# Moving twenty subtractions from VectorE to GpSimd in the attention of a hybrid decoder

## The chip, the cores and the metric

The kernel runs on one core of one Trainium2 chip. The metric is the device time of one execution in microseconds; lower is better. A core has five engines with queues of their own, each worked through in order: PE (TensorE, matrix products and transposes), DVE (VectorE), ACT (ScalarE), POOL (GpSimd) and SP (here only DMA issues). An instruction that needs another engine's result waits for a semaphore and holds up all that is queued behind it on its own engine.

## The reference

Two layers over 512 tokens of width 1024, all in float32. Layer 0 is a gated short convolution and a squared-ReLU MLP. Its result is normalised and projected once to keys and values. Layer 1 is a sparse attention with 16 heads in 4 groups, each head 64 wide, and another MLP. The attention has three branches that share the queries: compressed blocks, selected blocks and a window. With 512 tokens the selection takes all blocks, so both of the latter are full causal attention. Cut to the attention:

```
logit_c = einsum('bqghd,bngd->bqghn', qt, k_cmp) + bias_c         # 31 compressed keys
p_c = softmax(where(valid_c, logit_c, NEG_INF)) * has_any
o_c = einsum('bqghn,bngd->bqghd', p_c, v_cmp)
...                                                               # the same for selection and window
o = gt[..., 0:1] * o_c + gt[..., 1:2] * o_s + gt[..., 2:3] * o_w
x = x + o.reshape(B, S, N_HEADS * HEAD_DIM) @ w_o
```

v_cmp comes out of a small MLP (phi) over blocks of 32 tokens: `silu(flat @ w1) @ w2`.

## The kernel before

Each float32 operand of a product is split into two float16 pieces, the high one rounded from the value and the low one the remainder. A product is then three matmuls: high by high, high by low, low by high (`mm3`, lines 356 to 359). The splitting costs two elementwise instructions for each operand: ACT writes the high piece, and DVE subtracts it from the value (`split_to`, lines 377 to 382). Weights arrive by DMA in pieces (`wst`), and are split ahead of their use in the same way (lines 203 and 204).

The kernel is written for a tile scheduler: the order within each engine's queue and the semaphores come out of its plan, from the order in which the program states the work, the buffers that a tile name has (`bufs`) and what the planner holds each instruction to cost.

The attention is a list of items. A `Full` item is one group, one block of 128 queries, one branch (selection or window) and one to four heads; a `Cmp` item is two groups and one block of 128 queries in the compressed branch. There are 8 `Cmp` items: four for groups 0 and 1, put into the items of group 2, and four for groups 2 and 3, put into those of group 3. Each item has five stages, which the main loop states some items apart (`lead = {1: 2, 2: 3, 3: 4, 4: 6}`):

- st0: the logits on PE into bank "b"; DVE adds the bias into `at_s` (3 buffers), and ACT takes the exponential into `at_p`. A `Full` item gets sum and minimum in one DVE instruction (line 1021). A `Cmp` item adds (1089), reduces to the maximum (1091), subtracts it (1092), then exponential (1097) and sum (1099).
- st1: PE transposes the probabilities into one of two "c" banks (lines 1029, 1104); ACT copies the high piece out (1032, 1108).
- st2: DVE makes the low piece (1035, 1111), after which the bank is free.
- st3: the product with the values (1048 to 1050, 1120 to 1122), and its scaling by DVE into `o_t` (966), which POOL adds to the output `o` (968, 971).
- st4: where both parts of a group's block are there, `finish` has PE transpose `o` into a "c" bank (982), and `split_to` makes the pieces of the turned output in the tile `big` (378 and 380). `finish` handles one group, 256 columns, or two at once, 512. `finished` counts the blocks done of each group.

Between the items a background generator runs the projections: raw keys and values, `phi`, the queries of groups 1 to 3 (`queries`, where DVE scales them at line 703, ACT makes the high pieces at 800 and POOL the low ones at 801), and the output projection of groups 0 and 1 once all their blocks are finished. The output projection of groups 2 and 3 closes the attention. At the end of `phi(1)` the compressed values are spread over four heads by a mask (892) and split into `VC` by `split_to`.

Of the kernel before, what the change touches and what calls it, by code (L numbers as in the profile page):

```python
# [10 lines left out]
F32 = mybir.dt.float32  # L11
F16 = mybir.dt.float16
AF = mybir.ActivationFunctionType
OP = mybir.AluOpType
# [34 lines left out]
def body(ctx, tc, x, rel_bias, norm_mix, norm_mlp, mlp_w1, mlp_w2, a_w_in, a_conv_w, a_w_out,  # L49
# [3 lines left out]
    PE, ACT, DVE, POOL = nc.tensor, nc.scalar, nc.vector, nc.gpsimd  # L53
# [11 lines left out]
    def bank(tag, shape=(128, 512)):  # L65
        n = {"a": 2, "b": 2, "c": 2, "d": 1, "e": 1}[tag]
        return psum.tile(list(shape), F32, name=tag, bufs=n)
# [159 lines left out]
    def drain(gen):  # L227
        for _ in gen:
            pass
# [144 lines left out]
    def ftile(name, bufs=2, n=S):  # L374
        return wk[0].tile([128, n], F32, name=name, bufs=bufs)

    def split_to(hi, lo, src, scale=1.0):
        ACT.activation(hi, src, AF.Copy, scale=scale)
        if scale == 1.0:
            DVE.tensor_tensor(lo, src, hi, op=OP.subtract)  # L380
        else:
            DVE.scalar_tensor_tensor(lo, src, scale, hi, op0=OP.mult, op1=OP.subtract)
# [24 lines left out]
    for p in range(4):  # L407
# [55 lines left out]
        for dst in (pc, pu, pb):  # L463
# [7 lines left out]
            for m in range(2):  # L471
                ch = 2 * p + m
                if dst is pc:
                    if m == 0:
                        tmps = []
                    t = ftile("cv_t", 2)
# [177 lines left out]
    with pool("attn") as ap:  # L654
# [8 lines left out]
        VC = ap.tile([128, 2, G, 4, 64], F16, name="VC")  # L663
# [169 lines left out]
        def phi(which):  # L833
            kr = KRs[which]
            ph = [bank("a"), bank("a")]
            for quarter in range(4):
                w = next_piece()
                cv = ahead_fine()
                for c in range(4):
                    cc = 4 * quarter + c  # L840
                    at = 64 * (cc % 8) + cc // 8
                    rhs = [kr[:, hl, 0:5, at:at + 31] for hl in range(2)]
                    for m in range(2):
                        o = ph[m][:, 0:155].rearrange("p (g j) -> p g j", g=5)
                        mm3(o, [u[:, c, m * 128:(m + 1) * 128] for u in w], rhs, cc == 0, cc == 15)
                        next(cv, None)
                    yield 0.42
                drain(cv)
            hs = ap.tile([128, 2, 2, G, 32], F16, name="phi_h", bufs=1)
            DVE.memset(hs[:, :, :, :, 31:32], 0.0)  # L850

            for m in range(2):
                bias = ap.tile([128, 2], F32, name="phi_b", bufs=2)
                ACT.activation(bias[:, 0:1], ph[m][:, 124:125], AF.Copy)
                ACT.activation(bias[:, 1:2], ph[m][:, 124:125], AF.Copy, scale=0.5 / (SW * SK))
                t = ap.tile([128, G, 31], F32, name="phi_t", bufs=2)
                v = ph[m][:, 0:124].rearrange("p (g j) -> p g j", g=4)
                ACT.activation(t, v, AF.Tanh, bias=bias[:, 1:2], scale=0.5 / (SW * SK))
                ACT.activation(t, t, AF.Identity, bias=ones)
                DVE.scalar_tensor_tensor(t, v, bias[:, 0:1], t, op0=OP.add, op1=OP.mult)  # L860
                split_to(hs[:, m, 0, :, 0:31], hs[:, m, 1, :, 0:31], t, 0.5 * SR / (SW * SK))
            for _ in range(4):
                yield
            w = next_piece()
            if which == 0:
                pk = bank("e")
                w2 = [ap.tile([128, 2, 2, 64], F16, name=f"phi_w2{i}") for i in range(2)]
                for i in range(2):
                    for d in range(2):
                        DVE.tensor_copy(w2[i][:, :, d], w[i])  # L870
                for m in range(2):
                    mm3(pk[:, 0:128], [u[:, m].rearrange("p a b -> p (a b)") for u in w2],
                        [hs[:, m, i].rearrange("p g j -> p (g j)") for i in range(2)], m == 0, m == 1)
                split_to(KC[:, 0], KC[:, 1], pk[:, 0:128].rearrange("p (g j) -> p g j", g=4), SK / (SR * SW))
                yield
            else:
                pv = bank("e")
                hd = ap.tile([128, 4, S], F16, name="kr_hl", bufs=1).rearrange(
                    "p (m i) (g h n) -> p m i g h n", m=2, g=G, h=4)
                for m in range(2):  # L880
                    for i in range(2):
                        DVE.tensor_copy(hd[:, m, i], hs[:, m, i][:, :, None, :].to_broadcast([128, G, 4, 32]))
                for g in range(4):
                    o = pv[:, g * 64:(g + 1) * 64]
                    for m in range(2):
                        lh = [hd[:, m, i, g].rearrange("p h n -> p (h n)") for i in range(2)]
                        PE.matmul(o, lh[0], w[0][:, m], start=m == 0, stop=False)
                        PE.matmul(o, lh[0], w[1][:, m], start=False, stop=False)
                        PE.matmul(o, lh[1], w[0][:, m], start=False, stop=m == 1)
                for g in range(4):  # L890
                    t = ftile("at_s", 3)[:, 0:256].rearrange("p (h d) -> p h d", h=4)
                    DVE.tensor_tensor(t, pv[:, None, g * 64:(g + 1) * 64].to_broadcast([128, 4, 64]),
                                      hmask[:, :, None].to_broadcast([128, 4, 64]), op=OP.mult)
                    split_to(VC[:, 0, g], VC[:, 1, g], t)
                yield
            drain(ahead())

# [75 lines left out]
        def finish(g, n, qb, tag="c"):  # L973

            nonlocal ot
            if ot is None:
                o16 = ap.tile([128, 2, 8, S], F16, name="big", bufs=1)
                ot = (o16[:, 0], o16[:, 1])
            p = bank(tag)
            for j in range(n):  # L980
                for i in range(2):
                    PE.transpose(p[:, (2 * j + i) * 128:(2 * j + i + 1) * 128],
                                 og[g // 2, qb][:, (g + j) % 2, i * 128:(i + 1) * 128], ident)
            d = [u[:, 2 * g:2 * (g + n), qb * 128:(qb + 1) * 128] for u in ot]
            split_to(d[0], d[1], p[:, 0:n * 256].rearrange("p (i q) -> p i q", i=2 * n))
            for j in range(n):
                finished[g + j] += 1
            if finished[0] == finished[1] == 4:
                done.add("o1")

        finished = [0] * 4
# [74 lines left out]
        class Cmp:  # L1066
# [8 lines left out]
            def st0(self):  # L1075
                gp, qb, n = self.gp, self.qb, self.n
                if (gp, qb) == (0, 3):
                    done.add("cmp0")
                s = bank("b")[:, 0:256].rearrange("p (h n) -> p h n", h=8)
                for j in range(8):  # L1080
                    g, h = 2 * gp + j // 4, j % 4
                    q = Qs[g][:, h, qb * 128:(qb + 1) * 128]
                    PE.matmul(s[:, j, :n], q, KC[:, 0, g, :n], start=True, stop=False)
                    PE.matmul(s[:, j, :n], q, KC[:, 1, g, :n], start=False, stop=True)
                lg = ftile("at_s", 3)[:, 0:256].rearrange("p (h n) -> p h n", h=8)
                i = 8 * qb + 7
                tc_ = TC[gp].rearrange("p g h n -> p (g h) n")
                tv = tc_[:, :, i::-1] if i - n < 0 else tc_[:, :, i:i - n:-1]
                DVE.tensor_tensor(lg[:, :, :n], s[:, :, :n], tv, op=OP.add)
                mx = ap.tile([128, 8], F32, name="c_m", bufs=2)  # L1090
                DVE.tensor_reduce(mx, lg[:, :, :n], axis=mybir.AxisListType.X, op=OP.max)
                DVE.tensor_tensor(lg[:, :, :n], lg[:, :, :n], mx[:, :, None].to_broadcast([128, 8, n]),
                                  op=OP.subtract)
                self.p = ftile("at_p", 3)[:, 0:256].rearrange("p (h n) -> p h n", h=8)
                if n < 32:
                    POOL.memset(self.p[:, :, n:], 0.0)
                ACT.activation(self.p[:, :, :n], lg[:, :, :n], AF.Exp, bias=zero, scale=1.0 / SL)
                self.l = ap.tile([128, 8], F32, name="c_l", bufs=4)
                DVE.tensor_reduce(self.l, self.p[:, :, :n], axis=mybir.AxisListType.X, op=OP.add)
# [109 lines left out]
    with pool("hidden_b") as hp:  # L1209
# [5 lines left out]
        for half in range(2):  # L1215
            nc.gpsimd.dma_start(fng[half], bass.AP(tensor=final_norm.tensor, offset=final_norm.offset + half * S,
                                                   ap=[[0, 128], [1, S]]))
# [159 lines left out]
```

## Time and profile before

| | us |
|---|---|
| runs before, median of 3 (lowest to highest) | 1114.18 (1113.89 to 1116.89) |
| the profiled execution | 1114.68 |
| its span, first to last instruction | 1112.8 |
| PE, DVE, ACT, POOL busy | 1093.5, 869.8, 572.5, 62.4 |

The first half of the span, to about 530 us, is layer 0. The attention lies from about 530 to 790 us, and the second MLP behind it. A row of a wait reads: who waited, for whom, total us, how often, the longest. A group row reads: source line, engine, operation, output and inputs by the program's names, shapes, count; busy time in us and mean ns of one; idle time of the engine just before them and what ended it. A timeline row reads: start, duration, engine, line, operation; in brackets the idle time before it. A stretch row has, for each engine, the busy us and the number of instructions, and then the granted TensorE clock (1.00 is full), the busy share of the DMA engines and GB/s. PE's matmuls overlap and their ends are modelled.

### The profile page before, as it was taken

What the parts mean: (1) busy time and instruction counts of PE and PEld (TensorE: products, weight loads), DVE (VectorE), ACT (ScalarE), POOL (GpSimd) and SP (SyncE); (2) the same over time, 40 slices, a digit from 0 to 9 for tenths busy, and PEclk for the clock granted to TensorE, in tenths of its full rate; (3) what the DMA queues carried; (4) which work ended last, traced back from release to release, by engine and by line L of the source; (5) the groups of instructions that cost most, each with busy time, mean ns of one, the idle gap of its engine ahead of it and who ended that gap; (6) DMA issues with size and microseconds to landing.
All of it is one profiled execution on the core that took longest, in us unless ns stands there. A gap on an engine that the chain in (4) does not pass through costs nothing.

```text
span 1112.8 us, 20136 instructions
## 1 busy us (share of the span) xinstructions
PE 1093.5 (98%) x8004; PEld 696.9 (63%) x8004; DVE 869.8 (78%) x1630; ACT 572.5 (51%) x923; POOL 62.4 (6%) x79
## 2 busy tenths in 40 slices
PE   9999999999999999999998999899999999999997
PEld 4444444446884448875767676676444788444896
DVE  5755457987988677969588889897998698865876
ACT  4522235555343444447578787775755434343353
POOL 1000000000000000000102021212000000000021
PEclk9999999999999999999999999999999999999999
DMA  6433335543334333313334241111653333330221
GB/s 215 133 97 102 107 96 151 155 129 100 110 117 121 102 96 107 103 34 108 117 97 135 69 127 59 39 39 58 189 152 114 96 114 114 114 95 1 86 86 77
DMA packets 149565, 115.75 MB, mean 104 GB/s; under 512 B 8684, under 2 KB 146624, under 8 KB 149472
## 3 DMA queue, kind: packets, MB, share of 16 engines
q1 hardware_dynamic: 146624, 109.14, 32.3%
q10 hardware_dynamic: 2464, 4.70, 1.4%
q8 instruction: 63, 1.03, 0.4%
q0 software_dynamic: 384, 0.63, 0.2%
q14 instruction: 30, 0.25, 0.1%
HBM read 110.22 MB, written 2.14 MB: 101 GB/s over the span
## 4 chain that ended last, share of the span: by engine, by line
PE 86%; DVE 7%; ACT 4%; issue 2%; POOL 1%; DMA 1%; SPq 0%; DVEq 0%; ACTq 0%
PE a L583 8%; PE c L583 7%; PE a L358 6%; PE a L359 6%; PE a L357 6%; PE b L583 6%; PE c L359 6%; PE c L358 6%; PE c L357 6%; PE b L359 6%; PE b L358 5%; PE b L357 5%; PE d L583 4%; PE e L583 2%; PE c L1029 2%
## 5 line engine op out<-in xcount | busy, mean ns | idle before, releaser
L203 ACT ACTIVATE whi<-wst 128x1024 f16<-128x1024 f32 (+3 forms) x172 | 144.3, 854 | 188.0 <-PE b L358 66.8
L204 DVE SCALAR_TENSOR_TENSOR wlo<-wst,whi 128x1024 f16<-128x1024 f32 (+3 forms) x172 | 170.0, 999 | 44.8 <-ACT whi L203 44.3
L583 PEld LDWEIGHTS <-whi 128*128 128x128 f16 x1768 | 173.0, 98 | 20.5
L359 PEld LDWEIGHTS <-wlo 128*128 128x128 f16 x1024 | 100.3, 98 | 111.5 <-issue 0.5
L358 PEld LDWEIGHTS <-whi 128*128 128x128 f16 x1024 | 100.2, 98 | 108.7 <-issue 2.8
L357 PEld LDWEIGHTS <-whi 128*128 128x128 f16 x1024 | 100.3, 98 | 107.7 <-issue 0.9
L190 ACT ACTIVATE whi<-wst 128x1792 f16<-128x1792 f32 x64 | 108.5, 1700 | 109.5 <-DVE wst L188 47.5
L191 DVE SCALAR_TENSOR_TENSOR wlo<-wst,whi 128x1792 f16<-128x1792 f32 x64 | 129.3, 2023 | 14.0 <-ACT whi L190 14.0
L188 DVE TENSOR_TENSOR wst<-wst 128x256 f32<-128x256 f32 x256 | 96.1, 428 | 20.1 <-DMA wst<-mlp_w_dram 18.5
L534 DVE TENSOR_TENSOR rl<-ml_z,rh 128x1792 f16<-128x1792 f32 x32 | 64.8, 2026 | 44.7 <-ACT rh L533 44.7
L583 PEld LDWEIGHTS <-wlo 128*128 128x128 f16 x884 | 86.5, 98 | 10.5 <-issue 0.2
L533 ACT ACTIVATE rh<-ml_z 128x1792 f16<-128x1792 f32 x32 | 54.3, 1696 | 57.3 <-DVE ml_z L532 57.3
L1023 ACT ACTIVATE at_p<-at_s,at_m 128x384 f32<-128x384 f32 (+3 forms) x128 | 70.8, 554 | 22.2 <-DVE at_m L1021 20.7
L359 PE MATMUL b<-xsh,wlo 128*128 128x512 f16 x208 | 78.8, 379 | 0.0
L358 PE MATMUL b<-xsl,whi 128*128 128x512 f16 x208 | 78.8, 379 | 0.0
L357 PE MATMUL b<-xsh,whi 128*128 128x512 f16 x208 | 78.7, 379 | 0.0
L357 PE MATMUL c<-xsh,whi 128*128 128x512 f16 x192 | 72.8, 379 | 0.0
L358 PE MATMUL c<-xsl,whi 128*128 128x512 f16 x192 | 72.8, 379 | 0.0
L359 PE MATMUL c<-xsh,wlo 128*128 128x512 f16 x192 | 72.8, 379 | 0.0
L583 PE MATMUL a<-rh,whi 128*128 128x256 f16 x256 | 69.1, 273 | 0.0
L583 PE MATMUL a<-rh,wlo 128*128 128x256 f16 x256 | 69.1, 273 | 0.0
L583 PE MATMUL c<-rh,wlo 128*128 128x256 f16 x252 | 68.7, 273 | 0.0
(329 smaller groups left out, 2570.7 us busy)
## 6 DMA issues: line engine op xcount, KB each, us to landing
wst<-mlp_w_dram SPq DMA_DIRECT2D x256, 256.0 KB, 3.4
wst<-a_w_in_dram SPq DMA_DIRECT2D x18, 512.0 KB, 3.6
wst<-w_kv_dram SPq DMA_DIRECT2D x12, 512.0 KB, 3.5
T<-ext_d ACTq DMA_DIRECT2D x4, 1056.0 KB, 5.8
wst<-a_w_out_dram SPq DMA_DIRECT2D x8, 512.0 KB, 3.4
wst<-b_w_qg_dram SPq DMA_DIRECT2D x8, 512.0 KB, 3.6
wst<-b_w_o_dram SPq DMA_DIRECT2D x8, 512.0 KB, 3.4
wst<-a_w_in_dram SPq DMA_DIRECT2D x7, 384.0 KB, 4.8
```

Source lines behind the costliest of these rows:

```text
L188: DVE.tensor_tensor(b[:, :, o], b[:, :, x], b[:, :, y], op=e)
L190: ACT.activation(hi, b[:, :, 1:], AF.Copy, scale=sc)
L191: DVE.scalar_tensor_tensor(lo, b[:, :, 1:], sc, hi, op0=OP.mult, op1=OP.subtract)
L203: ACT.activation(hi[:, s:e], w, AF.Copy, scale=sc)
L204: DVE.scalar_tensor_tensor(lo[:, s:e], w, sc, hi[:, s:e], op0=OP.mult, op1=OP.subtract)
L357: PE.matmul(ps, w[0], xs[0], start=start, stop=False)
L358: PE.matmul(ps, w[0], xs[1], start=False, stop=False)
L359: return PE.matmul(ps, w[1], xs[0], start=False, stop=stop)
L533: ACT.activation(rh[0][:, p], z[:, 1:8], AF.Copy)
L534: DVE.tensor_tensor(rh[1][:, p], z[:, 1:8], rh[0][:, p], op=OP.subtract)
L583: mm = PE.matmul(acc7[i], wl if n == 1 else wh, xl if n == 2 else xh, stop=c == closes[i] and n == 2, start=c == 0 and n == 0 and not othe ...
L1023: ACT.activation(self.p[:, w], lg[:, w], AF.Exp, bias=mn[:, j:j + 1], scale=-1.0, accum_out=l[:, br * 4 + h:br * 4 + h + 1])
```

## The change

Three places.

- The low halves of the compressed values: POOL subtracts instead of DVE. ACT's high half stays.
- The low halves of the turned outputs in `finish`: unless the pair of groups (0 and 1, or 2 and 3) has with this call more than 6 of its 8 blocks done, ACT writes the high piece, then a second copy of the values in float32 to a new tile `o_f` with one buffer, and POOL subtracts. The later calls of a pair keep the old way. The count is raised before the test.
- The subtraction of the row maximum in the compressed items: POOL instead of DVE.

```diff
@@ -891,7 +891,8 @@
                     DVE.tensor_tensor(t, pv[:, None, g * 64:(g + 1) * 64].to_broadcast([128, 4, 64]),
                                       hmask[:, :, None].to_broadcast([128, 4, 64]), op=OP.mult)
-                    split_to(VC[:, 0, g], VC[:, 1, g], t)
+                    ACT.activation(VC[:, 0, g], t, AF.Copy)
+                    POOL.tensor_tensor(VC[:, 1, g], t, VC[:, 0, g], op=OP.subtract)
                 yield
@@ -982,9 +983,17 @@
             d = [u[:, 2 * g:2 * (g + n), qb * 128:(qb + 1) * 128] for u in ot]
-            split_to(d[0], d[1], p[:, 0:n * 256].rearrange("p (i q) -> p i q", i=2 * n))
             for j in range(n):
                 finished[g + j] += 1
+            src = p[:, 0:n * 256].rearrange("p (i q) -> p i q", i=2 * n)
+            pair_of = finished[g // 2 * 2:g // 2 * 2 + 2]
+            if sum(pair_of) > 6:
+                split_to(d[0], d[1], src)
+            else:
+                t = ap.tile([128, 512], F32, name="o_f", bufs=1)[:, 0:n * 256].rearrange("p (i q) -> p i q", i=2 * n)
+                ACT.activation(d[0], src, AF.Copy)
+                ACT.activation(t, src, AF.Copy)
+                POOL.tensor_tensor(d[1], t, d[0], op=OP.subtract)
             if finished[0] == finished[1] == 4:
                 done.add("o1")
@@ -1089,8 +1098,8 @@
                 DVE.tensor_reduce(mx, lg[:, :, :n], axis=mybir.AxisListType.X, op=OP.max)
-                DVE.tensor_tensor(lg[:, :, :n], lg[:, :, :n], mx[:, :, None].to_broadcast([128, 8, n]),
-                                  op=OP.subtract)
+                POOL.tensor_tensor(lg[:, :, :n], lg[:, :, :n], mx[:, :, None].to_broadcast([128, 8, n]),
+                                   op=OP.subtract)
                 self.p = ftile("at_p", 3)[:, 0:256].rearrange("p (h n) -> p h n", h=8)
```

In the built program the order of all engines is the same up to the compressed values and again after the attention; in between the scheduler states PE's, DVE's and ACT's instructions in another order.

## The prediction

> **What bounds the kernel now.** First the page: span and busy time by engine.
>
> ```profile
> span 1112.8 us, 20136 instructions
> PE 1093.5 (98%) x8004; PEld 696.9 (63%) x8004; DVE 869.8 (78%) x1630; ACT 572.5 (51%) x923; POOL 62.4 (6%) x79
> ```
>
> TensorE (PE) bounds the whole: 98% busy. The change adds or removes no matmul (the built program only reorders them from the first compressed item on), so it can only move time in which PE waits, or runs at a lower clock. It touches the attention from the compressed values on, whose first low half starts at 674.2 us, to the last moved output, turned at 759.83 (both rows below). The second view is the busy time by stretch, cut there and around the one dip that the page's slices hide.
>
> ```profile
> core 0: us, PE busy (x) PEld busy (x) DVE busy (x) ACT busy (x) POOL busy (x), PEclk, DMA share, GB/s
> 674.00:700.00 26.00, 25.02 (x283) 17.83 (x281) 25.62 (x87) 20.20 (x56) 6.55 (x7) 1.00 0.13 42
> 700.00:712.00 12.00, 9.15 (x87) 6.54 (x86) 9.36 (x29) 9.85 (x27) 5.33 (x5) 0.86 0.14 45
> 712.00:764.00 52.00, 51.37 (x614) 37.58 (x612) 50.38 (x156) 37.65 (x107) 9.17 (x14) 1.00 0.14 42
> ```
>
> In these 90 us DVE works 25.62 + 9.36 + 50.38 = 85.4 us, 95%; ACT 67.7, POOL 21.1. PE idles 0.98 + 2.85 + 0.63 = 4.5 us. The granted clock of 0.86 in the middle row is 12 x 0.14 = 1.7 us lost besides. That is what a relief of DVE can win: 4.5 + 1.7 = 6.2 us. The third view, the waits of PE in this stretch, says who ended the idle time:
>
> ```profile
> PE a L357 <- ACT big L378: 1.4, 1, 1.4
> PE c L982 <- DVE at_pl L1035: 1.3, 2, 1.1
> PE c L1104 <- DVE big L380: 0.5, 1, 0.5
> PE c L1029 <- DVE at_pl L1035: 0.4, 2, 0.2
> PE c L1104 <- ACT at_p L1097: 0.2, 1, 0.2
> ```
>
> 1.3 + 0.5 + 0.4 = 2.2 us end with DVE, each time a copy out of the two "c" banks that PE wants next; 1.4 us end with ACT. The fourth view, the timeline, shows how the two long ones arise, where the last group's queries come out:
>
> ```profile
> 699.96 1.29 DVE L703 TENSOR_TENSOR at_s<-a,rb 128x512 f32<-128x512 f32 x2
> 701.05 2.58 ACT L800 ACTIVATE Q<-at_s 64x512 f16<-64x512 f32 x4
> 701.16 0.69 DVE L1035 SCALAR_TENSOR_TENSOR at_pl<-c,at_ph 128x512 f16<-128x512 f32 x1
> 701.99 0.63 PE L982 MATMUL c<-ident,o 128*128 128x128 f32 x4 [1.10 <-DVE at_pl L1035]
> 704.15 0.59 ACT L378 ACTIVATE big<-c 128x512 f16<-128x512 f32 x1
> 704.22 0.42 DVE L1021 CUSTOM_DVE_ANT_0 at_s<-b,T 128x256 f32<-128x256 f32 x1 [1.23 <-POOL Q L801]
> 704.79 0.38 PE L357 MATMUL a<-big,whi 128*128 128x512 f16 x1 [1.44 <-ACT big L378]
> ```
>
> DVE comes to the low half at 701.16 only after the queries' 1.29 us, and PE stands 1.10 us for it. Then ACT copies the queries for 2.58 us, comes late to the turned output, and PE stands 1.44 us for the first output projection.
>
> **What is removed.** DVE's groups in the stretch 674 to 764, and the source line of the subtraction:
>
> ```profile
> L380 DVE TENSOR_TENSOR big<-c,big 128x512 f16<-128x512 f32 x5 | 3.4, 687 | 0.1
> L380 DVE TENSOR_TENSOR big<-c,big 128x256 f16<-128x256 f32 x4 | 1.7, 421 | 0.6 <-ACT big L378 0.5
> L380 DVE TENSOR_TENSOR VC<-at_s,VC x4: 416/418/420, 674.2 to 677.0; 128x256 f16<-128x256 f32 x4
> L1092 DVE TENSOR_TENSOR at_s<-at_s,c_m x8: 217/322/418, 678.1 to 748.6; 128x64 f32<-128x64 f32 x2, 128x128 f32<-128x128 f32 x2, 128x192 f32<-128x192 f32 x2, 128x256 f32<-128x256 f32 x2
> ```
>
> The condition counts finished blocks of a pair of groups after this one: over 6 of 8 stays as it was. The first pair turns four outputs of 512 columns, of which three move. The second turns seven; four of 256 and one of 512 move, the last two (256 each) stay. DVE loses 4 x 0.687 + 4 x 0.421 + 4 x 0.418 + 8 x 0.322 = 2.75 + 1.68 + 1.67 + 2.58 = 8.7 us, a tenth of its work here.
>
> **What is added.** ACT gets one more copy out of PSUM for each moved output, because POOL is given an f32 copy in SBUF. POOL gets 8 + 4 + 8 subtractions.
>
> ```profile
> L378 ACT ACTIVATE big<-c 128x512 f16<-128x512 f32 x5 | 3.0, 596 | 0.4 <-PE c L982 0.4
> L378 ACT ACTIVATE big<-c 128x256 f16<-128x256 f32 x5 | 1.9, 374 | 1.1 <-PE c L982 1.1
> L971 POOL TENSOR_TENSOR o<-o,o_t 128x256 f32<-128x256 f32 x9 | 7.3, 806 | 14.9 <-DVE o_t L966 14.7
> L971 POOL TENSOR_TENSOR o<-o,o_t 128x512 f32<-128x512 f32 x5 | 6.7, 1348 | 22.2 <-DVE o_t L966 22.2
> L1096 POOL MEMSET at_p<- 128x64 f32 x2 | 0.3, 151 | 3.6 <-PE c L1029 2.4 <-ACT at_ph L1108 1.2
> ```
>
> ACT: 4 x 0.596 + 4 x 0.374 = 3.9 us, on 67.7 of 90. I count nothing for it: 22 us of ACT's idle time cover it, and the bank is then freed by ACT's second copy at once, where DVE's turn had a queue before it. Without that cover the 3.9 us would be its price. POOL: 4 x 1.348 + 8 x 0.806 = 11.8 us for outputs and values. For a subtraction of 64 to 256 columns there is no POOL row: not below the memset's 0.151, not above 0.806 at 256. The two rows of L971 lie 0.542 apart for 256 columns, so their line gives 0.40 at 64 and 0.81 at 256; I take 0.6, 4.8 us in all. POOL goes from 21.1 to some 38 of 90 us: it has room, if its order lets it.
>
> A second price is that POOL and DVE slow each other:
>
> ```profile
> 684.23 0.68 DVE L204 SCALAR_TENSOR_TENSOR wlo<-wst,whi 128x512 f16<-128x512 f32 x1
> 684.39 1.65 POOL L971 TENSOR_TENSOR o<-o,o_t 128x512 f32<-128x512 f32 x1 [4.01 <-DVE o_t L966]
> 685.49 1.10 DVE L204 SCALAR_TENSOR_TENSOR wlo<-wst,whi 128x512 f16<-128x512 f32 x1
> ...
> L204 DVE SCALAR_TENSOR_TENSOR wlo<-wst,whi 128x512 f16<-128x512 f32 x10 | 7.1, 715 | 0.0
> L1056 DVE TENSOR_TENSOR rl<-rl,GT 128x8 f32<-128x8 f32 x7 | 1.9, 268 | 0.0
> L1126 DVE TENSOR_TENSOR rlc<-rlc,GT 128x8 f32<-128x8 f32 x8 | 1.3, 164 | 0.0
> ```
>
> The weight split that starts inside POOL's 1.65 takes 1.10, the one that started ahead of it 0.68. Over the stretch that is 10 x (0.715 - 0.68) + 7 x (0.268 - 0.164) = 1.1 us beside 21 us of POOL; 17 us more make 0.9 us. So DVE's net relief is 8.7 - 0.9 = 7.8 us. [...]
>
> **What of it reaches PE.** DVE is busy 25.62 of the 26 us before 700, so it brings the low halves later than PE could use them. With 5 us less before 700 (values, four subtractions, three outputs: 1.67 + 1.29 + 2.06) the waits that end with DVE shrink: I take the whole 2.2. The bounds are 0 and 2.2. The 1.4 behind ACT stays: the fourth output keeps the old way, and ACT's four copies of the queries stand before it still. The built program keeps that order of ACT: pieces of output three, exponentials, queries, output four.
>
> The half clock comes on top. Where PE idles 2.41 of 10 us it kept its clock; where it idled 2.85 it lost it:
>
> ```profile
> 600.00:610.00 10.00, 7.59 (x96) 5.36 (x94) 9.95 (x26) 8.44 (x29) 0.73 (x1) 1.00 0.77 237
> 700.00:710.00 10.00, 7.15 (x65) 5.07 (x64) 8.33 (x25) 8.85 (x25) 5.33 (x5) 0.83 0.01 2
> ```
>
> Without the 1.1 at 700.9 PE would idle 1.75 there, under the 2.41, so I let the dip go: 1.7 us, between 0 and 1.7 (a new dip elsewhere would cost the same 1.7). [...]
>
> At the end of attention the last moved output is turned at 759.83 and first read at 765.10:
>
> ```profile
> 759.83 0.60 PE L982 MATMUL c<-ident,o 128*128 128x128 f32 x4
> 765.10 0.38 PE L357 MATMUL c<-big,whi 128*128 128x512 f16 x1
> ```
>
> Two ACT copies and POOL's 1.35 are 0.60 + 0.60 + 0.60 + 1.35 = 3.2 us after 759.83: 763.0, 2.1 us ahead. It costs nothing; if that cover were gone, up to 1.35.
>
> Sum: 2.2 + 1.7 = 3.9 us. The profiled execution took 1114.68 us (span 1112.8 and 1.9 around it): 1110.8. The median of the three is 1114.18, 0.5 lower: 1110.3 us, 0.35% less. A measurement of this kernel can tell about 0.3%, 3.3 us, from no change.
>
> **Rivals.** *The relief stays on DVE* (chance 0.25). PE's long waits come from the order (queries first, then the low half), not from DVE's load. For it: the order around the queries is the same in the built program, and ACT's 9.85 of 12 us leaves little. Against it: DVE had no idle time before 700. Then only the 0.5 at L1104 and some of the 0.4 go and the dip stays: about -0.7, 1113.5 us.
>
> *POOL's queue takes DVE's place* (0.25, the slower one). at_s has three buffers, and now POOL holds them. The fourth value product, the first compressed logits and the next full item wait for POOL's low halves of the values: 4 x 0.806 in a row from 674.2 end at 677.4, where DVE's last ended too (677.0 + 0.42). Then each compressed item's exponential waits for a subtraction that stands in POOL's queue, behind sums of 1.348. What stands for it in the rows of waits and of DVE's groups:
>
> ```profile
> ACT at_p L1097 <- DVE at_s L1092: 3.0, 4, 1.6
> ...
> L1035 DVE SCALAR_TENSOR_TENSOR at_pl<-c,at_ph 128x512 f16<-128x512 f32 x28 | 19.1, 685 | 0.8 <-ACT at_ph L1032 0.7
> L1035 DVE SCALAR_TENSOR_TENSOR at_pl<-c,at_ph 128x384 f16<-128x384 f32 x8 | 4.4, 553 | 0.0
> ```
>
> ACT already waits 3.0 us for it, in order, and holds back what comes next: up to 1.35 + 0.3 more on each of eight, 13 us at the worst. Against it: the item's transposes come two items later; the stretch has 28 + 8 full items by the rows of L1035 and 8 compressed ones, so 90 / 44 = 2 us each, 4 us of cover; PE waited 0.2 for it. It decides from the point at which the subtraction comes over 4 us late. If half of the eight cost 1 us of PE each, it is +4: 1118.2 us; a second half-clock window would add 1.7.
>
> That the change doesn't do what it says I leave out: the built program has 20 more subtractions on POOL, 8 more ACT copies and 20 fewer instructions on DVE.
>
> **How the numbers follow.** Forecast 0.50, no gain 0.25, slower 0.25. The forecast's own range is 1108.0 (all 6.2) to 1111.5. Matmul ends are modelled, so some waits may not show; I go to 1106.5 below. Above, the range takes in the slower case to 1118.0. Faster by over 0.3% 0.50, within 0.25, slower 0.25.
>
> **What would show it.** Right: DVE some 77 us busy between the values and 764; no wait of "c" transposes on L1035 over 0.3; no clock under 1.00 there; POOL near 38. Wrong: PE waiting on POOL's c_m subtraction or on ACT's second copy; DVE idle at at_s behind POOL; the dip still there, or two.

## The result, and the profile after

| | before | after |
|---|---|---|
| median of 13 runs each, us (lowest to highest) | 1114.14 (1112.07 to 1116.89) | 1117.02 (1116.26 to 1119.87) |
| the profiled execution, us (its span) | 1114.68 (1112.8) | 1117.59 (1115.8) |

The changed kernel is slower: the ratio is 1.0034, 95% interval 1.0026 to 1.0041, some 3.8 us (the medians lie 2.9 us apart). The page after:

```profile
span 1115.8 us, 20159 instructions
PE 1091.3 (98%) x8004; PEld 695.8 (62%) x8004; DVE 865.6 (78%) x1610; ACT 575.6 (52%) x931; POOL 76.3 (7%) x99
```

The work moved as stated: DVE is down 4.2 us, ACT up 3.1, POOL up 13.9. Where it landed, by stretches as before:

```profile
674.00:700.00 26.00, 22.97 (x252) 16.02 (x250) 22.80 (x65) 18.34 (x49) 13.63 (x17) 1.00 0.19 63
700.00:712.00 12.00, 8.58 (x107) 6.76 (x108) 10.65 (x38) 11.59 (x35) 6.51 (x6) 1.00 0.01 1
712.00:764.00 52.00, 50.31 (x590) 36.90 (x588) 46.35 (x145) 39.77 (x113) 13.54 (x22) 1.00 0.13 42
```

DVE now has idle time, 90 - 79.8 = 10.2 us instead of 4.6, and PE has more of it too: 3.03 + 3.42 + 1.69 = 8.1 us where it had 4.5. The half clock of 1.7 us is gone from this profile, and still the span is 3.0 us longer. The waits of PE in 674 to 766:

```profile
PE c L983 <- DVE at_pl L1044: 2.4, 2, 1.3
PE d L1057 <- DVE o_t L967: 1.7, 1, 1.7
PE c L1113 <- ACT o_f L995: 1.6, 3, 0.7
PE c L1038 <- DVE at_pl L1044: 1.2, 1, 1.2
PE b L1092 <- DVE at_s L1098: 0.8, 1, 0.8
```

(In the changed kernel the attention's lines stand 1 to 9 further down: 1044 is the low half that was 1035, 983 the turned output, 1113 the compressed transposes, 995 the new f32 copy.) 2.4 + 1.2 = 3.6 us end with the very low halves that were to come sooner; 1.6 us are new, PE waiting on ACT's second copy for the "c" bank. Of the 2.4 us, 1.30 are the old wait in the queries' stage (at 704.96, where the queries' 1.28 us of products still stand ahead of the low half on DVE), and 1.09 are new. Both places, in the timeline, the new one first:

```profile
689.70 1.15 POOL L996 TENSOR_TENSOR big<-o_f,big 128x512 f16<-128x512 f32 x1
689.80 1.60 DVE L204 SCALAR_TENSOR_TENSOR wlo<-wst,whi 128x512 f16<-128x512 f32 x1
...
691.32 0.68 DVE L1044 SCALAR_TENSOR_TENSOR at_pl<-c,at_ph 128x512 f16<-128x512 f32 x1
...
692.15 0.63 PE L983 MATMUL c<-ident,o 128*128 128x128 f32 x4 [1.09 <-DVE at_pl L1044]
...
702.94 1.28 DVE L703 TENSOR_TENSOR at_s<-a,rb 128x512 f32<-128x512 f32 x2
704.96 0.63 PE L983 MATMUL c<-ident,o 128*128 128x128 f32 x4 [1.30 <-DVE at_pl L1044]
```

At the new place DVE has a weight split in its queue ahead of the low half. The split takes 1.60 us beside POOL's subtraction (0.68 when it is alone), and PE stands 1.09 us. The split stands there because the planner, presumably since it now holds DVE for less loaded, has written another order: 127 of PE's matmuls stand elsewhere in the built program's queue (the two traces show over 110), and ACT's and DVE's queues are changed from the first compressed item on. Two things were thus changed at once, who does the work and the order of the queues. The experiments take them apart.

### The profile page after: what moved, and what is told of

It reads as the page before. It is cut to its first block, busy times and chain, and to the rows that moved or that the text cites. A ratio compares the mean times of both kernels' runs of the same rounds, so it can differ in the third digit from the quotient of the medians.

```text
span 1115.8 us, 20159 instructions
## 1 busy us (share of the span) xinstructions
PE 1091.3 (98%) x8004; PEld 695.8 (62%) x8004; DVE 865.6 (78%) x1610; ACT 575.6 (52%) x931; POOL 76.3 (7%) x99
## 4 chain that ended last, share of the span: by engine, by line
PE 85%; DVE 6%; ACT 4%; issue 2%; POOL 1%; DMA 1%; SPq 0%; DVEq 0%; ACTq 0%
PE a L583 8%; PE c L583 7%; PE a L358 6%; PE a L357 6%; PE a L359 6%; PE b L583 6%; PE c L357 6%; PE c L358 6%; PE c L359 6%; PE b L359 5%; PE b L358 5%; PE b L357 5%; PE d L583 4%; PE e L583 2%; PE c L1038 2%
## 5 line engine op out<-in xcount | busy, mean ns | idle before, releaser
L583 PE MATMUL c<-rh,whi 128*128 128x256 f16 x252 | 68.7, 273 | 0.0
```

The source lines that it names most:

```text
L583: mm = PE.matmul(acc7[i], wl if n == 1 else wh, xl if n == 2 else xh, stop=c == closes[i] and n == 2, start=c == 0 and n == 0 and not othe ...
```

## Experiments

Each ratio is to runs of the kernel before on the same chip. "Pinned" means that the order of the engines' queues in the attention is given by a list, through dependencies that order instructions of one engine and cost no semaphore:

```
for eng, ranks in order.items():          # PE, DVE, ACT; in runs 13 to 15 and 17 POOL too
    made = [i for i in instructions if i.engine == eng]
    for x, y in zip(ranks, ranks[1:]):
        tc.add_manual_dep(made[y], made[x].name, NoSync, reason="order of before")
```

The built programs then have the queue order asked for, except where a moved subtraction or second copy has to stand somewhere new. Such a kernel's lines stand some 40 to 47 further down than before, so tiles are the safer names.

**1. The changed operations in the order of before.** Edit: the changed kernel, with PE, DVE and ACT pinned to the queues of before.

> All 20 moved subtractions and 8 second copies of the change, but TensorE, VectorE and ScalarE issue in the attention in the order that they had before (pinned by dependencies that cost no semaphore); only GpSimd's 20 instructions and ScalarE's second copies are new. Theory A (the order: the planner, whose estimates have changed, put weight splits ahead of low halves and restated 127 matmuls, and that costs the 3 us): the loss goes, and what DVE was relieved of shows, 1110 to 1114 us. Theory B (GpSimd: its subtractions come late, hold at_s and slow DVE's two-input instructions): the loss stays, 1116 to 1118 us, with waits of ACT on at_s L1101 and of DVE on VC as in the changed kernel. Theory C (ScalarE's second copies hold the bank): 1116 to 1118, with PE waiting on o_f.

Measured: 1115.43 us, 1.0012 (1.0003 to 1.0021). Between the theories: about two thirds of the loss go with the order (1.0034 to 1.0012, some 2.5 us), and a third stays with the operations. What PE waits for now:

```profile
PE a L395 <- ACT big L416: 2.2, 1, 2.2
PE d L1095 <- ACT at_ph L1079: 0.7, 1, 0.7
PE c L1076 <- DVE at_pl L1082: 0.4, 2, 0.2
PE c L1021 <- DVE rlc L1172: 0.3, 1, 0.3
PE c L1151 <- ACT o_f L1033: 0.3, 1, 0.3
PE c L1021 <- DVE at_pl L1082: 0.3, 1, 0.3
PE c L1151 <- ACT at_p L1144: 0.2, 1, 0.2
```

The waits on DVE have shrunk as predicted, 1.3 to 0.3 at the turned output. But the wait that I had let stay, 1.4 us behind ACT, has become 2.2, with 0.7 more behind ACT just ahead of it. ACT's queue in the stage ahead, in the kernel before and then in this one:

```profile
696.42 0.60 ACT L378 ACTIVATE big<-c 128x512 f16<-128x512 f32 x1
696.91 1.14 ACT L203 ACTIVATE whi<-wst 128x512 f16<-128x512 f32 x2
698.04 0.40 ACT L1023 ACTIVATE at_p<-at_s,at_m 128x128 f32<-128x128 f32 x1
```

```profile
697.23 0.59 ACT L1032 ACTIVATE big<-c 128x512 f16<-128x512 f32 x1
697.71 0.60 ACT L1033 ACTIVATE o_f<-c 128x512 f32<-128x512 f32 x1
698.19 1.16 ACT L241 ACTIVATE whi<-wst 128x512 f16<-128x512 f32 x2
699.23 0.41 ACT L1070 ACTIVATE at_p<-at_s,at_m 128x128 f32<-128x128 f32 x1
...
702.23 1.94 ACT L838 ACTIVATE Q<-at_s 64x512 f16<-64x512 f32 x3
```

The second copy of the third output (`o_f`, 0.60) stands in a queue that has no gap from there to the queries' copies. Those start at 702.23 instead of 701.05, 1.18 later. PE's matmuls ahead of that place, the same ones in both traces, start 0.46 later than before, so 0.7 us are this queue's; PE's wait behind it is 0.8 longer.

**2. The old operations in the new order.** Edit: the kernel before, pinned to the queues of the changed one.

> The kernel before, every subtraction still on DVE, but TensorE, VectorE and ScalarE pinned to the order that the changed kernel has. Theory A (order): 1117 us or more, since DVE then has the bad order and its old work too. Theories B and C (GpSimd, second copies): 1114 us, as before.

Measured: 1120.79 us, 1.0059 (1.0046 to 1.0071). The order by itself costs 6.6 us with the old operations; in that order the moved work is worth something (1.0059 to 1.0034), since there PE waits for DVE in many places. That the order was planned for a relieved DVE is my reading of it.

**3. The turned outputs alone**, values and maxima left on DVE, the planner free.

> Only the turned outputs are moved (8 second ACT copies, 8 subtractions on GpSimd), values and maxima stay on DVE; the planner orders freely. Theory A: anything from 1112 to 1117, by the order it happens to get. Theory B with the outputs as the culprit, or C: 1116 to 1117; B with the maxima or values as culprits: 1113 to 1114.

Measured: 1118.15 us, 1.0037 (1.0024 to 1.0050): as slow as the whole change, in an order that is again the planner's own.

**4. The maxima alone**, planner free.

> Only the subtraction of the row maximum in the eight compressed items is moved to GpSimd; the planner orders freely. Theory A: anything from 1112 to 1117, by its order. Theory B with the maxima as culprits: 1115 to 1118, ACT waiting for at_s L1092 well over the 3.0 us of before. Theory C: 1114.

Measured: 1114.92 us, 1.0009 (1.0000 to 1.0018): little or nothing, although the planner reordered PE's queue between 678 and 763 us here too. So not every new order costs much.

**5. Values and maxima in the order of before** (outputs as before, pinned).

> The values' low halves and the maxima's subtractions on GpSimd, the turned outputs as before, in the order of before. In the pinned run of the whole change PE waited 2.2 us instead of 1.4 for the turned output's copy behind the queries, because ScalarE's second copy of the output ahead of it had pushed its queue back. Theory C' (the second copies eat what DVE's relief gives): without them 1113 to 1114 us, level with before or a little under it. Theory B (GpSimd's lateness or its contention with DVE costs): 1115, as the pinned whole.

Measured: 1114.06 us, 1.0003 (0.9994 to 1.0012). Level: in this order GpSimd's lateness and its contention with DVE cost nothing that shows, and DVE's relief by these twelve gives nothing either.

**6. The outputs in the order of before** (values and maxima as before, pinned).

> Only the turned outputs moved (8 second copies on ScalarE, 8 subtractions on GpSimd), in the order of before. Theory C': 1115 to 1116 us, the wait behind the queries at 2.2 us. Theory B with values and maxima as culprits: 1113 to 1114.

Measured: 1115.65 us, 1.0013 (1.0004 to 1.0021), with the same wait as in the first run. The loss that the operations cause is in the outputs.

```profile
PE a L389 <- ACT big L410: 2.2, 1, 2.2
PE d L1088 <- ACT at_ph L1072: 0.6, 1, 0.6
```

**7. The relief alone.** Edit, pinned to the order of before:

```diff
-                    split_to(VC[:, 0, g], VC[:, 1, g], t)
+                    ACT.activation(VC[:, 0, g], t, AF.Copy)
+                    POOL.memset(VC[:, 1, g], 0.0)
...                                             # the moved outputs likewise, without o_f
-                DVE.tensor_tensor(lg[:, :, :n], lg[:, :, :n], mx..., op=OP.subtract)
-                ACT.activation(..., AF.Exp, bias=zero, scale=1.0 / SL)
+                ACT.activation(..., AF.Exp, bias=zero, scale=1e-30 / SL)
```

> In the order of before, DVE's 20 subtractions are left out and nothing takes their place: the low halves of the values and of the seven moved outputs are zeros that GpSimd writes ahead of time, and the compressed items' logits go unreduced into an exponential of near zero scale. It leaves that part of the computation out, and shows what the relief of DVE by 8.7 us is worth to PE at most. The prediction took 2.2 us of waits and 1.7 us of half clock: then 1110 us. If the relief stays on DVE, as the pinned whole suggests: 1113 to 1114 us.

Measured: 1113.03 us, 0.9995 (0.9986 to 1.0004). In this order, to have these subtractions for nothing at all is worth 0.6 us, 1.6 at the most and perhaps nothing, since the interval takes in 1. (The change moves eight outputs; the seven in the expectation is a slip.) Its busy time and PE's waits, in the queries' stage:

```profile
700.00:712.00 12.00, 9.01 (x82) 6.31 (x79) 9.36 (x27) 9.85 (x27) 5.34 (x5) 0.86 0.14 45
```

```profile
PE a L395 <- ACT big L416: 1.7, 1, 1.7
PE c L1021 <- DVE at_pl L1080: 0.8, 1, 0.8
```

DVE and ACT do in these 12 us exactly what they did before (9.36 and 9.85): none of the twenty lies in the stage. PE's two waits are 0.8 and 1.7 instead of 1.1 and 1.4: what it gains at the one it loses at the next.

**8. ACT's copy ahead of the queries.** Edit to the kernel before, pinned: ACT's queue `Q Q Q Q at_ph big` becomes `Q Q at_ph big Q Q`.

> The kernel before with its own operations and order, but on ScalarE the exponentials' half and the copy of the fourth turned output go ahead of the last two copies of the queries (two instructions moved ahead of two). If PE's 1.4 us in the queries' stage is ScalarE's order, it goes, and the half clock there may go with it: 1111 to 1113 us. If the queries are what the stage waits for, 1114 or more.

Measured: 1114.35 us, 1.0002 (0.9993 to 1.0010). The 1.4 us behind ACT went and came back behind DVE:

```profile
PE d L1088 <- DVE o_t L1006: 1.4, 1, 1.4
PE c L1022 <- DVE at_pl L1075: 1.3, 2, 1.1
```

`o_t` stands in DVE's queue behind biased logits that wait 1.24 us for an `at_s` buffer, which POOL's low halves of the queries hold. POOL's queue was not pinned, and the planner put one output sum ahead of the last of these.

**9 and 10. The order by halves.** Edit: the changed kernel, pinned to the order of before up to about 725 us and then to its own, and the other way about.

> All of the changed kernel's operations; TensorE, VectorE and ScalarE in the order of before up to about 725 us (past the queries' stage), then in the changed kernel's own. The whole change measured +0.34%, the same operations wholly in the old order +0.12%. If the late part of the new order costs (turned outputs' second copies right ahead of compressed transposes, PE waiting 1.6 us on o_f there), 1116.5 to 1117 us; if the early part does (weight splits ahead of low halves around 690 us), 1115 to 1115.5.

> The mirror of the last: the changed kernel's own order up to about 725 us, then the order of before. If the late part of the new order costs, 1115 to 1115.5 us; if the early part does (splits ahead of low halves; it lost 3 us by 697 us and had regained them by 714), 1116.5 to 1117.

Measured: 1117.54 us, 1.0032 (1.0021 to 1.0044), and 1116.62 us, 1.0029 (1.0020 to 1.0039). Each half of the new order costs nearly as much as the whole, 0.20 and 0.17% above the first run's 1.0012. So neither theory alone holds. By the ratios the two costs do not add up, but the clock is mixed into them: a mean granted clock of 0.998 or more, which goes with no half clock in the queries' stage (last section), was had by none of run 1's 11 executions, 1 of run 9's 6, 4 of run 10's 9 and 9 of the changed kernel's 13. The others took 1115.4 us on average in run 1, 1117.3 in run 9, 1117.4 in run 10 and 1119.4 in the changed kernel (only four executions): about 2 us for each half and 4 for both. In the late half the loss has a row: run 9 has the wait on the second copy as the changed kernel has it, where the old order (run 1) had 0.3 of it, and from 714 to 764 us its matmuls fall back by 1.5 us against the kernel before, those of run 1 not at all.

```profile
PE c L1153 <- ACT o_f L1035: 1.6, 3, 0.7
```

**11 and 12. The queries' stage by hand.** Edit to the kernel before, pinned, and the same with values and maxima on POOL:

```
ACT  Q Q Q Q at_ph big                              ->  Q Q at_ph big Q Q
DVE  q q at_pl at_s at_s rl at_s* o_t at_pl big at_s ->  q at_pl q at_s at_s rl o_t at_pl big at_s* at_s
```

(`q` is the scaled queries, `at_s*` the biased logits that wait for POOL.)

> The kernel before with its own operations; in the queries' stage ScalarE's copy of the fourth turned output goes ahead of the last two copies of the queries, and on DVE the low half that PE waits 1.10 us for goes ahead of the queries' second product, and the scaling of the output (o_t) with what follows it ahead of the biased logits that wait for a buffer held by GpSimd. If PE's waits there are the order of the queues and not DVE's load: they fall from 2.85 us to under 1.5, 1112 to 1113 us. If the waits only move on again, as with ScalarE's copy alone: 1114.

> The same order by hand, with the values' low halves and the maxima's subtractions on GpSimd besides (the part of the change without second copies). If relief of DVE is worth something once the queues stand right: a further 0.5 to 1 us, 1111.5 to 1112.5. If relief is worth nothing to PE: as the last run.

Measured: 1113.55 us, 1.0000 (0.9991 to 1.0009), and 1113.98 us, 1.0001 (0.9992 to 1.0010). In its trace run 11 was 2.7 us ahead of before just ahead of 708.85 us (some 1.1 of it because the trace of before is at half clock there), and lost 1.8 at the next step:

```profile
707.33 0.42 DVE L1061 CUSTOM_DVE_ANT_0 at_s<-b,T 128x256 f32<-128x256 f32 x1 [1.80 <-POOL Q L841]
```

```profile
PE c L1069 <- DVE at_pl L1075: 2.2, 3, 1.9
```

The next low half stands behind the next logits, which wait for POOL's last subtraction of the queries; the planner had put an output sum ahead of that one.

**13, 14 and 15. Once more by hand.** As 11, with the next `at_pl` ahead of those logits and POOL's four subtractions of the queries kept together (13); the same with the twenty subtractions left out as in run 7 (14); the same as 13 with values and maxima on POOL (15).

> As the queries' stage by hand, and besides the next low half on DVE goes ahead of the biased logits that wait for GpSimd's copy of the queries (1.80 us there), with GpSimd's four subtractions of the queries kept together. If the order of the queues is the cause of PE's waits: the 1.9 us that had moved to the next transposes goes too, 1111 to 1112.5 us. If GpSimd's 4.8 us for the queries bounds the stage: the wait moves on once more, 1113.5 to 1114.

> The order of the last run, and DVE's 20 subtractions left out with nothing in their place (low halves of values and moved outputs zero, the compressed items' logits unreduced into an exponential of near zero scale; that part of the computation is left out). If relief is worth something once the order is right: at least 1 us under the last run. If PE's remaining waits are not DVE's load: within 0.5 us of it.

> The order of the last two runs, with the values' low halves and the maxima on GpSimd (a correct kernel). Between the two: at best the gain of the run without the subtractions, at worst 0.3 to 0.5 us above the run with all of them on DVE, as in the order of before.

Measured: 1112.23 us, 0.9986 (0.9977 to 0.9995); 1110.97 us, 0.9976 (0.9967 to 0.9985); 1112.93 us, 0.9993 (0.9984 to 1.0002). Run 13 has all the subtractions where they were and is ahead of both kernels. PE idles 12 - 10.27 = 1.73 us in the queries' stage instead of 2.85:

```profile
700.00:712.00 12.00, 10.27 (x111) 6.78 (x108) 11.18 (x33) 11.00 (x31) 6.06 (x6) 1.00 0.15 46
```

```profile
PE c L1070 <- DVE at_pl L1076: 0.8, 3, 0.4
PE c L1023 <- DVE at_pl L1076: 0.7, 2, 0.5
...
PE a L398 <- ACT big L419: 0.3, 1, 0.3
```

A part of this gain is the clock: all 33 executions of these three runs have a mean granted clock of 0.998 or more, where most of those of before have less (last section). Against the executions of before with such a clock, 1113.2 us, run 13 gains 1.0. In that order the subtractions for nothing (14) are worth 0.10% more, a little over 1 us. The intervals of 13 and 14 overlap, but the two ran side by side, and 8 of the 11 executions of 14 are faster than the fastest of 13. Values and maxima on POOL (15) do not get it: 0.7 us above run 13, more than the 0.3 to 0.5 expected at worst.

**16. The third output back on DVE.** Edit to run 1's kernel:

```diff
-            if sum(pair_of) > 6:
+            if sum(pair_of) > 6 or g < 2 and sum(pair_of) > 4:
```

> The whole change in the order of before, but the third turned output, whose second ScalarE copy stands right ahead of the copies of the queries, goes back to DVE. Theory C' (this one copy makes the loss of 0.12%, through the wait behind the queries of 2.2 instead of 1.4 us): 1114 us, level with before, the wait back at 1.4. If the loss is spread over the second copies or lies with GpSimd: 1115 to 1115.5.

Measured: 1113.93 us, 1.0001 (0.9992 to 1.0009); the wait is back at its old size, and so is that of 1.1 us behind DVE. The other 19 moved subtractions and 7 second copies stay, and in this order they together cost and give nothing that shows. The intervals of this run and of runs 1 and 6 just overlap, and the third output's subtraction on POOL went with its copy; that it is the copy rests on ACT's queue as run 1's trace shows it.

```profile
PE a L395 <- ACT big L416: 1.4, 1, 1.4
PE c L1021 <- DVE at_pl L1082: 1.1, 1, 1.1
```

**17. One split behind.** Edit to the changed kernel, pinned to its own order: on DVE the weight split at 689.80 and the low half behind it change places.

> The changed kernel in its own order on every engine, but for one pair: on DVE the weight split that stood ahead of the low half at 689.8 us goes behind it. If that split is what the early half of the order costs: PE's wait of 1.09 us there goes, 1115.5 to 1116 us. If the delay is made up by 714 us anyway, or lies in the order as a whole: 1116.5 to 1117, as the changed kernel.

Measured: 1117.52 us, 1.0029 (1.0019 to 1.0040), no difference from the changed kernel that can be told, and above both forecasts. In the trace the low half starts at 689.25, PE's 1.09 us wait there is gone (0.5 of another is left), and from 695 to 708 us PE is 0.6 us further than in the changed kernel, counted from 674. Then this execution has a granted clock of 0.75 in the queries' stage, twice the usual loss, so the one trace can't show what became of the 0.6. This split is a small part at most; the early half's cost was not brought down to single instructions.

## Why the prediction was wrong

**The step that failed first is "What of it reaches PE".** It took the whole 2.2 us of waits that end with DVE, because DVE was busy 25.62 of 26 us. Run 7 shows what the relief is worth in the order of before: 0.6 us, at most 1.6. The waits on DVE did shrink where the change was run in that order (run 1: those that end with DVE fell from 2.2 to 1.0 us), but PE got none of it, since those that end with ACT rose from 1.6 to 3.4. A DVE that is always busy is not thereby late where PE waits: the long wait lay in the queries' stage, in which none of the twenty instructions stands, and was set by three queues, the queries' products on DVE, their copies on ACT and their 4.8 us of subtractions on POOL, whose `at_s` buffers DVE waits for (1.23 us at 704.22). Runs 8, 11 and 13 show this: moved one by one, the waits went from ACT to DVE's `o_t` to the next low half, and only with all three queues rearranged did PE gain (0.14%). The two waits of the stage, DVE's low half and then ACT's copy, show it by themselves: 1.1 + 1.4 us before, 0.3 + 2.2 in run 1, 1.1 + 1.4 in runs 5 and 16, 0.8 + 1.7 in run 7, 2.5 us each time. That is the first rival, "the relief stays on DVE", as a mechanism. Its price of 1113.5 us is near run 7's 1113.03, but the changed kernel was not that case. That the measured 1117.02 lies inside the range is luck: the range reached 1118.0 for the sake of POOL's queue, which was not the cause.

**The new order was priced at nothing.** I saw that the built program reorders matmuls and gave it no term. Run 1 against the changed kernel makes it 0.22%, some 2.5 us (about 4 among the executions with the lower clock, runs 9 and 10); it is the largest term of the result, and with the old operations it is 6.6 us (run 2). Why the order costs so much is shown by rows for the late half alone.

**ACT's 3.9 us were counted at nothing, for 22 us of idle time.** The average hid the place. In the order of before, seven of the eight second copies cost nothing that shows (run 16), and the one in a stretch where ACT had no gap cost some 0.12%, 1.3 us (runs 1, 6 and 16), of which 0.7 can be read off ACT's queue; a part of the rest goes with the clock (last section). The prediction knew that ACT was at 9.85 of 12 us in the next stretch, and named the wait of 1.4 us behind it as staying; in run 1 it grew to 2.2. In the changed kernel's own order that row is gone, and ACT's price has another: of the signs listed for a wrong forecast, PE waiting on its second copy came, 1.6 us. DVE idle at `at_s` behind POOL came too, 3.4 us instead of 1.2.

**The half clock** was tied to PE's idle time in the stage, with 2.41 us as a bound. That does not hold: the same stage ran at 1.00 in the changed kernel with 3.42 us idle. The forecast that the dip goes came true in part all the same, by luck: 9 of 13 executions of the changed kernel have the higher mean clock, and about a third of those of before (last section).

**POOL** went as forecast. It is 33.7 of 90 us busy, against 38 forecast:

```profile
L996 POOL TENSOR_TENSOR big<-o_f,big 128x256 f16<-128x256 f32 (+1 forms) x7 | 6.2, 879 | 11.1 <-ACT o_f L995 11.1
...
L1101 POOL TENSOR_TENSOR at_s<-at_s,c_m 128x64 f32<-128x64 f32 (+3 forms) x8 | 4.0, 504 | 4.9 <-DVE c_m L1100 2.3 <-DVE rlc L1134 2.1 <-DVE rl L1065 0.4
...
L895 POOL TENSOR_TENSOR VC<-at_s,VC 128x256 f16<-128x256 f32 x4 | 3.1, 805 | 4.8 <-ACT VC L894 4.8
```

0.504 for a maximum (0.6 taken), 0.805 for a value (0.806 taken). The slower rival, POOL's queue in DVE's place, is not what made it slower, though its 1118.2 us lies near: ACT waits 4.1 us for the subtracted maxima instead of 3.0, PE never for them (0.8 us of PE's waits are for the first biased compressed logits, behind POOL's values), and run 4 puts the maxima at 0.09%, run 5 values and maxima at 0.03%. Run 3 is as slow without either of them on POOL.

**DVE's net relief of 7.8 us** was too large. Leaving the twenty out lowered DVE's busy time over the span from 869.8 to 863.8 us (run 7), 6.0 and not 8.7; neighbours in its queue overlap, by 0.09 us at 701.16, and as much at each of the twenty would account for 1.8 of the 2.7 between. With POOL's work beside it, in the same order, it was 865.5 (run 1). So contention took some 1.7 us, not 0.9, by one execution of each. In the rows above the longest single hit is the split at 689.80: 1.60 us, 0.92 longer than alone (0.68); POOL's instruction of 1.15 us from 689.70 had 1.05 us to go when it started. By runs 5 and 16 (1.0003 and 1.0001) none of it shows in the time in the order of before.

## What to carry to other kernels

An engine's load over a stretch does not say what a relief is worth: it was worth something else in each order of the queues. Leaving out the same twenty was worth 0.6 us in the order of before and about 1.2 in the one of run 13, and moving them 2.8 in the planner's new one (run 2 to the changed kernel). Take the wait, list the queue ahead of the late instruction on each engine in turn, and see if the removed work stands in one of them. Count an added instruction at nothing only where its engine is idle at that place, not on average. Where a planner writes the order, price its new order as a part of the change, and pin the old one to tell the two apart. Compare the granted clock over all executions, since the order can change how often it falls (it fell in all 22 executions of runs 1 and 6 and in none of the 33 of runs 13 to 15, by the mean clock of each).

## What was not expected of the hardware

The dip to half clock in the queries' stage does not follow from how long PE idles there. The rows of the stage 700 to 712 us in run 1, run 5 and run 8:

```profile
700.00:712.00 12.00, 8.52 (x83) 6.04 (x82) 9.35 (x27) 10.54 (x32) 5.45 (x6) 0.86 0.04 10
```

```profile
700.00:712.00 12.00, 9.13 (x101) 6.27 (x100) 10.54 (x31) 10.66 (x29) 5.46 (x6) 1.00 0.14 43
```

```profile
700.00:712.00 12.00, 8.56 (x92) 6.17 (x93) 10.07 (x33) 10.55 (x31) 5.34 (x5) 1.00 0.04 10
```

PE idles 3.48, 2.87 and 3.44 us, at 0.86, 1.00 and 1.00; the kernel before had 0.86 at 2.85. The dip had one size here: in eight of the nine traces that have one the clock of the stage is 0.86 (in the kernel before, one half for 3.41 us), and in run 17 about twice as much is lost, at 0.75 in the stage and 0.99 from 712 to 764 us.

It comes and goes between executions of one kernel. In all 19 traces the mean granted clock of the execution is 0.998 or more without a dip in the stage and 0.997 or less with one, so this mean tells the two apart, though not without doubt, where there is no trace. Over 124 executions of the kernel before that were timed beside the experiments, 40 had 0.998 or more and took 1113.2 us on average, the other 84 1114.2: a dip goes with about 1 us, and one profile says little of how often it is there.

How often it comes went with the order of the queues in these runs, and some of the edits took it away. Free of it by this measure were 40 of 124 executions of before, 9 of 13 of the changed kernel, none of 22 of runs 1 and 6, 6 of 11 in each of runs 5, 8 and 16, and 54 of 55 of runs 11 to 15. The longest single wait of PE from 674 to 766 us goes some way with it: it is 2.2 us in runs 1, 3, 6 and 9 (1 of 33 free) and 0.6 us or less in runs 13 to 15 (33 of 33 free). But in runs 11 and 12 it is 1.9 us, and 21 of 22 are free. What decides stays open; the longest wait of PE in that stretch in any of the nine traces with a dip was 2.2 us.
